# A fused two-block transformer kernel: gates, spreads and mod gates through device memory, aligned small tiles, earlier context rows, later gate work

## The chip, the cores and the metric

The kernel runs on one core of a Trainium2 chip. Five engines work side by side, each through its own queue in order: TensorE (PE, matrix products into PSUM; PEld is its weight load), VectorE (DVE), ScalarE (ACT), GpSimd (POOL) and SyncE (SP, which here issues nearly all transfers between device memory and the on-chip memory SBUF). The metric is the device time of one launch in microseconds; the median of the runs is compared.

## What is computed

Two blocks of two layers each, on 512 rows of 1024 numbers, in float32. The first block mixes tokens by an mLSTM in chunks of 128 with gates per head, beside a sliding-window attention; a convolutional gated network follows. The second block takes a condition vector and 256 context rows, and mixes by pooling, neighbourhood attention with a bias and retention in both directions; a modulated, gated network follows. Cut to what the change touches:

```python
def mlstm_chunkwise(q, k, v, log_i, log_f):          # first block
    ...
    bc = jnp.cumsum(chunks(log_f), axis=-1)
    def step(carry, inp):
        C, n, m = carry
        q_, k_, v_, b_, li_ = inp
        dlog = b_[..., :, None] - b_[..., None, :] + li_[..., None, :]
        dlog = jnp.where(causal, dlog, -jnp.inf)
        inter = b_ + m[..., None]
        m_row = jnp.maximum(inter, jnp.max(dlog, axis=-1))
        w_intra = jnp.exp(dlog - m_row[..., None])
        w_inter = jnp.exp(inter - m_row)
        s = jnp.einsum('bhtd,bhsd->bhts', q_, k_) * w_intra
        ...
        ws = jnp.exp(ls - m_new[..., None])
def token_mixer(h, w_in, qk_conv_w, qk_conv_b, gate_bias, mh_norm_g, attn_sinks, w_out):
    z = h @ w_in
    ...
    log_i = gates[..., :MLSTM_HEADS]
    log_f = jax.nn.log_sigmoid(gates[..., MLSTM_HEADS:])
def modulate(t, shift, scale):                       # second block
    return t * (1 + scale) + shift
def neighborhood_attention(q, k, v, kc, vc, rpb, rows):
    ...
    s_loc = jnp.where(valid, s_loc + bias, NEG_INF)
def retention_chunks(q, k, v, log_gamma, state, with_outputs):
    ...
        s_new = s * c_dec[None, :, None, None] + jnp.einsum('bhcd,bhce->bhde', kb * k_dec[None, :, :, None], vb)
```

## The kernel before

**Products.** A float32 product is done as three products of split numbers (`mm3`, L435 to L437): a high part times a high part, high times low, low times high. Weights stream in: SP fetches a slab into `wr` (3 buffers, L359), ScalarE casts its high part to `wh` (L373), VectorE subtracts to get the low part `wl` (L374); 5 buffers each. Normed rows, turned so that features lie on partitions, stand as `nh` and `nl`. A row of the trace such as `mm<-nh,wh` names the two operands.

**Order.** The program is recorded by a planner: `later(delay, fn)` puts a step on a heap against `s.now`, a count of TensorE's planned nanoseconds, and while the weight products are recorded, the steps that are due are recorded between them. So the delays and the table `Q` of start times set each engine's order, and nothing is reordered on the chip. SP's queue is in order too: a transfer that waits for its data holds all fetches behind it.

**Temporaries.** Nearly every temporary is a tile of the tag `u`: a ring of 34 buffers. Some shapes of 516 and 528 columns use the same tag, so each buffer has 2112 bytes per partition, and a tile's start goes through eight values modulo 512 bytes. `wh`, `wl`, `nh`, `nl` start 32 bytes past a multiple of 512.

**Gates of the mLSTM (`gates`, twice, once a layer).** From 8 gate columns per row, TensorE turns 4x128 tiles (`ax<-ident,t`), VectorE copies them to rows of 4x512 (L910), and makes the running sums and maxima by scans (L918 and L923, with five short steps between and after); TensorE turns two of the results back (`ax<-ident,u` of 4x4 output). In `mlstm`, `spread` brings each head's row to 64 partitions by a matmul with a 0/1 matrix `sel2` (4 rows deep) and takes Exp from PSUM (L1080); `decay` makes a 128x512 matrix from one row by three matmuls (L1101 to L1103: minus the row's high part, minus its low part, plus a causal mask) and takes Exp per chunk (L1108).

**Second block.** `mod` makes the modulation columns `md`; `gate_bc` (6 calls) spreads a gate from columns to rows over all partitions by 16 matmuls each (`ax<-ident,md`) and two ScalarE copies. `early` loads the 256 context rows into `mraw` (L2012) when block two starts, and Norm squares them on ScalarE (L141). The neighbourhood bias comes into `mraw` tiles with a zero half; retention's six state steps (`step`, L1320 and L1321) go in one direction on VectorE and in the other on GpSimd.

Of the kernel before, what the change touches and what calls it, by code (L numbers as in the profile page):

```python
# [11 lines left out]
F32 = mybir.dt.float32  # L12
F32R = mybir.dt.float32r
AF = mybir.ActivationFunctionType
ALU = mybir.AluOpType
# [11 lines left out]
NU = 34  # L27
# [4 lines left out]
NW = 5  # L32
NM = 2
MOD_T = 2330
T_M = 30000
NRAW = 4
# [12 lines left out]
Q = {"swa": 2600, "ctx": 612, "na": 1218, "ret": 6600, "mod": 19000, "mod0": 30000.0, "cn": 18000, "gates": 1750, "fill": 11520, "na1": 1600, "na2": 6253, "na3": 2116, "sw1": 1400, "sw2": 3135, "sw3": 1250, "cx1": 1080, "cx2": 2160, "cx3": 1557}  # L49
# [155 lines left out]
class Net:  # L205
    def __init__(s, ctx, tc, a):
        s.tc, s.nc, s.a = tc, tc.nc, a
        s.sb = ctx.enter_context(tc.tile_pool(name="sb", bufs=1))
        s.ps = ctx.enter_context(tc.tile_pool(name="ps", bufs=1, space=bass.MemoryType.PSUM))
# [5 lines left out]
        s.mready = []  # L215
        s.modon = False
# [83 lines left out]

    def u(s, shape=(P, 512), dt=F32):
        x = s.sb.tile(list(shape), dt, tag="u", name=s.nm("u"), bufs=NU)
        return x
# [9 lines left out]
    def tag(s, tag, shape, bufs, dt=F32):  # L313
        return s.sb.tile(list(shape), dt, tag=tag, name=s.nm(tag), bufs=bufs)
# [318 lines left out]
    def ffn(s, l, up, dn, taps, groups, causal, bias, make_sinks, parts, early=None):  # L633
# [7 lines left out]
        for i in range(np_):  # L641
            f0, f1 = parts[i], parts[i + 1]
            if up == "up2" and i == np_ - 1:
                yield from s.until(lambda: len(s.mready) == 2)
# [4 lines left out]
            if early and i == np_ - 1:  # L649
                yield from s.until(lambda: 0 in s.mready)  # L650
                early()
# [103 lines left out]
    def consts1(s):  # L755
        nc = s.nc
        bf = mybir.dt.bfloat16
        s.identb = s.fix([P, P], "identb", bf)
        nc.vector.tensor_copy(s.identb, s.ident)
# [10 lines left out]
        s.nid4 = s.fix([4, 4], "nid4", F32R)  # L770
        nc.vector.tensor_scalar(out=s.nid4, in0=s.ident[:4, :4], scalar1=-1.0, scalar2=None, op0=ALU.mult)
        s.sel2 = s.fix([4, 2, P], "sel2")
        nc.sync.dma_start(s.sel2, s.a["sel2"])
        s.ones4 = s.fix([4, 512], "ones4")
        nc.vector.memset(s.ones4, 1.0)
        nc.vector.memset(s.ones4.rearrange("p (c t) -> p c t", t=P)[:, :, 0:1], 0.0)
# [7 lines left out]
    def consts3(s):  # L784
        nc = s.nc
        s.cos1 = s.sin1 = s.swm = s.sel2 = None
# [4 lines left out]
        s.bias = []  # L791
        for _ in range(2):
            bias = s.tag("mraw", [P, 1024], NRAW)
            nc.gpsimd.memset(bias, 0.0)
            s.bias += [bias[:, i * 512:i * 512 + 512] for i in range(2)]
# [1289 lines left out]
```

## Time and profile before

| | |
|---|---|
| median of 3 runs | 2862.58 us (2859.92 to 2866.8) |
| the profiled execution | 2865.19 us, of which span 2863.4 us |
| TensorE | 2762.5 us busy, 96% of the span |
| VectorE, ScalarE, GpSimd | 66%, 41%, 20% |
| mean granted TensorE clock | 0.983 of full speed |
| DMA | 300.68 MB, mean 105 GB/s |

TensorE's busy time counts a matmul until its modelled end, so it overlaps with the next one's start; the spacing of starts is what a matmul costs in a row of them. Granted clock 0.50 in a stretch means that the clock was at its lower level (1.2 GHz) all through it, 1.00 at its upper one (2.4 GHz).

### The profile page before, as it was taken

The numbers are of one execution on the slowest core, as the hardware profiler recorded it, in microseconds if no ns is written. First come the engines' busy times: TensorE is split into PE (matmuls) and PEld (weight loads), VectorE is DVE, ScalarE is ACT, GpSimd is POOL, SyncE is SP. The second block draws the span as 40 slices with busy tenths as digits, with TensorE's granted clock in tenths as the row PEclk, the third lists the DMA queues.
The fourth block names the chain that finished last, engine by engine and source line by source line (L and its number), as shares of the span: only waits on it lengthen the run. The fifth ranks groups of instructions, "written<-read, shape, count | busy, mean of one in ns | idle before, by whom it ended". The sixth has DMA issues, their size and how long they took to land.

```text
span 2863.4 us, 39056 instructions
## 1 busy us (share of the span) xinstructions
PE 2762.5 (96%) x14694; PEld 2316.3 (81%) x14694; DVE 1900.0 (66%) x3414; ACT 1175.6 (41%) x2112; POOL 559.0 (20%) x617
## 2 busy tenths in 40 slices
PE   8899999998999999999999999999999999999998
PEld 6678888876678887788788898888888888888887
DVE  6746867686468677767556777777755556664544
ACT  5445333344454333355443633223235443442433
POOL 3112000032120000036134211220202434201011
PEclk9889999999999999999999999999999999999999
DMA  4122544432134444433332333333212322333332
GB/s 162 55 70 89 169 143 129 152 92 81 45 99 141 143 151 137 141 122 99 104 96 77 91 107 114 103 115 116 89 61 80 117 75 73 96 110 96 96 96 66
DMA packets 106324, 300.68 MB, mean 105 GB/s; under 512 B 12180, under 2 KB 18200, under 8 KB 106136
## 3 DMA queue, kind: packets, MB, share of 16 engines
q1 hardware_dynamic: 105560, 297.14, 33.6%
q8 instruction: 116, 1.90, 0.3%
q10 hardware_dynamic: 576, 1.05, 0.1%
q14 instruction: 72, 0.59, 0.1%
HBM read 296.04 MB, written 2.10 MB: 104 GB/s over the span
## 4 chain that ended last, share of the span: by engine, by line
PE 81%; DVE 9%; ACT 4%; issue 2%; POOL 2%; DMA 1%; SPq 0%; POOLq 0%; DVEq 0%; ACTq 0%
PE mm L435 24%; PE mm L437 24%; PE mm L436 24%; PE ax L569 5%; PE ax L565 3%; DVE wl L374 2%; PE ax L577 1%; ACT u L173 1%; ACT wh L373 1%; POOL u L700 1%; DVE mjunk L835 1%; POOL t L560 1%; DVE u L605 1%; DVE u L1209 1%; DMA wr<-in_up_dram 0%
## 5 line engine op out<-in xcount | busy, mean ns | idle before, releaser
L373 ACT CAST wh<-wr 128x1024 fp32r<-128x1024 f32 (+2 forms) x455 | 461.7, 1017 | 598.3 <-PE mm L437 285.9
L435 PE MATMUL mm<-nh,wh 128*128 128x512 f32 (+1 forms) x1776 | 673.1, 379 | 3.6 <-DVE nh L185 3.6
L436 PE MATMUL mm<-nl,wh 128*128 128x512 f32 (+1 forms) x1776 | 667.7, 376 | 0.8 <-DVE nl L186 0.5
L437 PE MATMUL mm<-nh,wl 128*128 128x512 f32 (+1 forms) x1776 | 667.6, 376 | 0.0
L374 DVE TENSOR_TENSOR wl<-wr,wh 128x1024 fp32r<-128x1024 f32 (+2 forms) x455 | 570.7, 1260 | 109.3 <-ACT wh L373 108.9
L435 PE MATMUL mm<-wh,u 128*128 128x512 f32 (+1 forms) x1176 | 464.5, 395 | 6.8 <-ACT u L620 6.8
L605 DVE SCALAR_TENSOR_TENSOR u<-mm,vec,u 128x511 f32<-128x511 f32 (+2 forms) x440 | 305.8, 695 | 238.6 <-ACT u L600 161.8
L436 PE MATMUL mm<-wl,u 128*128 128x512 f32 (+1 forms) x1176 | 458.8, 390 | 2.5 <-DVE wl L374 2.4
L437 PE MATMUL mm<-wh,u 128*128 128x512 f32 (+1 forms) x1176 | 459.1, 390 | 1.4 <-DVE u L621 1.4
L435 PEld LDWEIGHTS mm<-nh,wh 128*128 128x128 f32 x1776 | 336.6, 190 | 66.1 <-issue 4.8
L437 PEld LDWEIGHTS mm<-nh,wl 128*128 128x128 f32 x1776 | 336.7, 190 | 61.0
L436 PEld LDWEIGHTS mm<-nl,wh 128*128 128x128 f32 x1776 | 337.0, 190 | 59.0 <-DVE nl L186 1.0
L435 PEld LDWEIGHTS mm<-wh,u 128*128 128x128 f32 x1176 | 221.8, 189 | 55.8 <-ACT u L620 7.7
L436 PEld LDWEIGHTS mm<-wl,u 128*128 128x128 f32 x1176 | 221.9, 189 | 50.0 <-DVE wl L374 4.4
L437 PEld LDWEIGHTS mm<-wh,u 128*128 128x128 f32 x1176 | 221.4, 188 | 49.4 <-DVE u L621 2.5
L435 PE MATMUL mm<-wh,nh 128*128 128x384 f32 (+2 forms) x512 | 193.6, 378 | 6.1 <-DVE nh L185 5.8
L565 PE MATMUL ax<-ident,u 128*128 128x128 f32 (+1 forms) x946 | 139.7, 283 | 57.3 <-DVE u L152 16.5
L437 PE MATMUL mm<-wh,nl 128*128 128x384 f32 (+2 forms) x512 | 184.0, 359 | 1.3 <-POOL nl L186 1.3
L436 PE MATMUL mm<-wl,nh 128*128 128x384 f32 (+2 forms) x512 | 184.0, 359 | 0.0
L565 PEld LDWEIGHTS ax<-ident,u 128*128 128x128 f32 (+1 forms) x946 | 109.6, 145 | 91.5 <-issue 30.9
L725 POOL TENSOR_TENSOR x<-x,u 128x512 f32<-128x512 f32 x64 | 102.5, 1602 | 352.2 <-DVE u L724 351.4
L560 POOL TENSOR_TENSOR t<-t,mhalf 128x1 f32<-128x1 f32 (+2 forms) x76 | 61.9, 817 | 528.4 <-DVE t L558 528.1
(262 smaller groups left out, 3760.0 us busy)
## 6 DMA issues: line engine op xcount, KB each, us to landing
wr<-in_up_dram SPq DMA_DIRECT2D x176, 512.0 KB, 3.9
mrow<-in_wmod_dram SPq DMA_DIRECT2D x192, 256.0 KB, 2.9
wr<-in_dn_dram SPq DMA_DIRECT2D x88, 512.0 KB, 4.0
wr<-in_wo_dram SPq DMA_DIRECT2D x56, 512.0 KB, 3.6
wr<-in_w2b_dram SPq DMA_DIRECT2D x56, 384.0 KB, 3.1
wr<-in_w2a_dram SPq DMA_DIRECT2D x39, 512.0 KB, 3.6
mraw<-in_nab_dram SPq DMA_DIRECT2D x36, 128.0 KB, 3.5
wr<-in_w1q_dram SPq DMA_DIRECT2D x8, 512.0 KB, 5.1
```

The lines of the kernel that those rows point to most:

```text
L173: nc.scalar.activation(m[:, j, :], src, AF.Identity, scale=n.g[:, k:k + 1], bias=n.b[:, k:k + 1])
L373: nc.scalar.copy(h[:, :n], raw[:, :n])
L374: s.wlo[i] = lambda: nc.vector.tensor_sub(lo[:, :n], raw[:, :n], h[:, :n].bitcast(F32))
L435: mm(ps, ah, bh, start=first, stop=False)
L436: mm(ps, ah, bl, start=False, stop=False)
L437: mm(ps, al, bh, start=False, stop=last)
L560: nc.gpsimd.tensor_tensor(out=r, in0=e, in1=s.mhalf[:, :n], op=ALU.pow)
L565: s.nc.tensor.transpose(out, in_, s.ident[:p, :p])
L569: s.nc.tensor.matmul(out, l, r, start=start, stop=stop, **kw)
L577: s.nc.tensor.matmul(out[q], l, r, start=start, stop=stop, tile_position=(0, i * 64))
L605: nc.vector.scalar_tensor_tensor(out=c[:, o], in0=ps[:, i], scalar=w[q], in1=c[:, o], op0=ALU.mult, op1=ALU.add)
L725: eng.tensor_add(x[:, c], x[:, c], o)
```

## The change

1. **Gates.** They start later (`Q["gates"]` 1750 to 16000). The turns go through device memory: `gates2` stores 8 pieces element by element into `grow`, `gates3` loads two 4x512 rows, `gates4` scans as before (with fewer tiles), `fin` stores five rows into `gfin`, `cols` loads 8 pieces element by element as columns, `ends` takes the Exp.
2. **mLSTM.** `bring` loads rows of `gfin` over 64 partitions, `spread` takes Exp in place; `bring_m` loads a row over 128 partitions, `mask` subtracts it from the causal mask on GpSimd, `decay` takes Exp in place. `sel2`, `nid4`, `identb`, `ones4` go.
3. **Mod gates.** `keep` stores the gate columns once (`mgate`), `gate_bc` loads them over 128 partitions; the two waits for `mready` become waits for `mgate`.
4. **Context rows** are loaded at planned 60000 ns instead of in `early`.
5. **Tiles.** The ring `u` has 31 buffers of 2048 bytes, aligned to 512; a new ring `ub` of 6 takes the wider shapes; `wh`, `wl`, `nh`, `nl` are aligned to 512; the bias tiles get a buffer of their own (`nab`), `mraw` goes from 4 to 2.
6. **Small.** The pads' memsets go from GpSimd to VectorE; the pool sums reuse a tile; `mod`'s scratch is ScalarE's `junk`.

```diff
-NU = 34
+NU = 31
+NB = 6
...
-NRAW = 4
+NRAW = 2
...
-Q = {... "gates": 1750, ...
+Q = {... "gates": 16000, ...
...
     def u(s, shape=(P, 512), dt=F32):
-        x = s.sb.tile(list(shape), dt, tag="u", name=s.nm("u"), bufs=NU)
-        return x
+        n = 1
+        for d in shape[1:]:
+            n *= d
+        if n > 512:
+            return s.sb.tile(list(shape), dt, tag="ub", name=s.nm("ub"), bufs=NB)
+        return s.sb.tile(list(shape), dt, tag="u", name=s.nm("u"), bufs=NU, align_bytes=512)
...
+            def keep():
+                gd = s.dram([2, 2, D], "mgate")
+                for w in range(2):
+                    for i in range(2):
+                        o = (3 * i + 2) * 8
+                        nc.sync.dma_start(gd[w, i].rearrange("(j p) -> p j", p=P), md[:, w, o:o + 8])
+                s.mgate[l] = gd
+            s.later(1200, keep)
...
     def gate_bc(s, l, w, part):
...
-                s.mmf(ps[:, j * P:(j + 1) * P], s.md[l][:, w, o:o + 1].to_broadcast([P, P]), s.ident)
...
-            nc.scalar.copy(g, ps)
+            row = s.mgate[l][w, part // 3, half * 512:half * 512 + 512]
+            s.nc.sync.dma_start(g, row.partition_broadcast(P))
...
-        s.later(6930, lambda: s.gates2(g3, lf3, got))
+        s.later(6000, lambda: s.gates2(g3, lf3, gd, got))
+    def gates2(s, g3, lf3, gd, got):
+        for i, src in enumerate((g3, lf3)):
+            for t in range(NT):
+                nc.sync.dma_start(gd[i * 4:i * 4 + 4, t * P:(t + 1) * P].rearrange("h p -> p h"), src[:, t, :4])
+        s.later(3000, lambda: s.gates3(gd, got))
+    def gates3(s, gd, got):
-            for t in range(NT):
-                s.tr(ps[:4, t * P:(t + 1) * P], src[:, t, :4])
             r = s.u((4, 512))
-            nc.vector.tensor_copy(r, ps[:4, :])
+            nc.sync.dma_start(r, gd[i * 4:i * 4 + 4])
+        s.later(2800, lambda: s.gates4(rows, got))
...
         def fin():
+            gr = s.dram([5, 4, 512], "gfin")
+            for i, x in enumerate((bm, a, m, wi, ws)):
+                nc.sync.dma_start(gr[i], x)
+            s.later(2600, lambda: cols(gr))
+        def cols(gr):
+            co = s.ti(32)
+                    nc.sync.dma_start(co[:, i * 16 + c * 4:i * 16 + c * 4 + 4],
+                                      gr[i, :, c * P:(c + 1) * P].rearrange("h p -> p h"))
+            s.later(2800, lambda: ends(gr, co))
...
+        def bring(hp):
+                    nc.sync.dma_start(w[i * 64:i * 64 + 64, :], gr[src, hp * 2 + i].partition_broadcast(64))
+        def bring_m(hp):
+                nc.sync.dma_start(w, gr[2, hp * 2 + i].partition_broadcast(P))
+            s.later(2800, lambda: mask(hp))
+        def mask(hp):
+                nc.gpsimd.tensor_sub(w, s.cmaskb, w)
         def spread(hp):
-                s.mmf(ps, s.sel2[:, hp, :], src)
-                nc.scalar.activation(w, ps, AF.Exp)
+                nc.scalar.activation(w, w, AF.Exp)
         def decay(h):
-            nc.tensor.matmul(ps, neg, mh, start=True, stop=False)
-            nc.tensor.matmul(ps, neg, ml, start=False, stop=False)
-            nc.tensor.matmul(ps, s.identb, s.cmaskb, start=False, stop=True)
...
+    def load_ctx():
         for i in range(2):
             x = s.tag("mraw", [P, D], NRAW)
             nc.sync.dma_start(x, a["ctx"][i * P:(i + 1) * P])
             cs.append(x)
+    s.later(60000, load_ctx)
```

In the changed program the lines of `mm3` are L447 to L449, transposes are L577 and `step` is L1357 and L1358.

On TensorE, in the mLSTM of layer 0 (`wh`, `wl` are weights, `nh`, `nl` normed rows), this stood before:

```order
L436 MATMUL mm_1459<-wl_1028,nh_109 128x512
L437 MATMUL mm_1459<-wh_1027,nl_110 128x512
L569 MATMUL ax_1468<-u_786,sel_158 128x512
L569 MATMUL ax_1472<-u_785,sel_158 128x512
L435 MATMUL mm_1460<-wh_1027,nh_109 128x512
```

and a little further on

```order
L565 MATMUL ax_1514<-ident_65,u_1495 128x128 x4
L1101 MATMUL ax_1521<-u_914,nid_156 128x512
L1102 MATMUL ax_1521<-u_915,nid_156 128x512
L1103 LDWEIGHTS identb_144
L1103 MATMUL ax_1521<-cmaskb_146,identb_144 128x512
```

After the change, weight products and transposes follow each other there:

```order
L449 MATMUL mm_1428<-wh_983,nl_112 128x512
L577 MATMUL ax_1501<-ident_67,u_1478 128x128 x4
L447 MATMUL mm_1429<-wh_983,nh_111 128x512
L448 MATMUL mm_1429<-wl_984,nh_111 128x512
L449 MATMUL mm_1429<-wh_983,nl_112 128x512
L447 MATMUL mm_1430<-wh_983,nh_111 128x512
```

The four-row matmuls are gone from between the weight products, which moved together.

On VectorE, in the attention stage of layer 0 (L1025 and its L1035, L1036, L581 are softmax steps, L1209 convolution taps), the gate steps L910 to L920 stood before between two of the softmax steps:

```order
L1028 TENSOR_TENSOR t_760<-small_82,t_758 128x2
L910 COPY u_773<-ax_768 4x512
L910 COPY u_780<-ax_775 4x512
L917 MEMSET t_789 4x1
L918 SCALAR_TENSOR_TENSOR u_782<-ones_160,u_780 4x512
L919 TENSOR_TENSOR u_783<-u_773,u_782 4x512
L920 COPY u_788<-u_782 4x3
L374 TENSOR_TENSOR wl_710<-wr_692,wh_709 128x1024
```

The same place after the change, where softmax, split and taps (now L1049, L386, L1246) follow each other:

```order
L1052 TENSOR_TENSOR t_744<-small_84,t_742 128x2
L386 TENSOR_TENSOR wl_694<-wr_676,wh_693 128x1024
L1077 COPY u_763<-ax_760 128x256
L1254 TENSOR_SCALAR u_679<-u_679 128x512
L1246 SCALAR_TENSOR_TENSOR u_770<-mm_681,vec_72,u_770 128x511
L1059 TENSOR_TENSOR t_732<-t_732,t_733 128x2
```

The gate steps stand now behind the last convolution taps of the stage (L1246 writing `u_986`):

```order
L593 TENSOR_SCALAR u_952<-u_952,t_956 128x256
L1246 SCALAR_TENSOR_TENSOR u_986<-mm_872,vec_72,u_986 128x509
L934 MEMSET t_1013 4x1
L935 SCALAR_TENSOR_TENSOR u_1010<-u_1012,u_981 4x512
L936 TENSOR_TENSOR u_979<-u_979,u_1010 4x512
```

On SP, the queue that feeds the weights (`wr`), slab fetches followed each other in this stage before:

```order
L359 DMA wr_1021<-in_w1o_dram 128x1024
L359 DMA wr_1127<-in_w1o_dram 128x1024
L359 DMA wr_1274<-in_wo_dram 128x1024
L359 DMA wr_1360<-in_wo_dram 128x1024
L359 DMA wr_1448<-in_wo_dram 128x1024
```

After the change the gates' stores and loads stand between them (`x4` is four such transfers):

```order
L371 DMA wr_879<-in_w1o_dram 128x1024
L912 DMA grow_821<-t_813 128x4x1 x4
L912 DMA grow_821<-t_815 128x4x1 x4
L371 DMA wr_977<-in_w1o_dram 128x1024
L920 DMA u_979<-grow_821 4x512
L920 DMA u_981<-grow_821 4x512
L371 DMA wr_1084<-in_w1o_dram 128x1024
L950 DMA gfin_1115<-u_1011 4x512
```

The slab fetches keep their order and now stand behind transfers that wait for VectorE.

## Rows read from the trace of the kernel before

**Rows 1.** The page, parts 1 and 4: busy us (share), the chain by engine.

```profile
PE 2762.5 (96%) x14694; PEld 2316.3 (81%) x14694; DVE 1900.0 (66%) x3414; ACT 1175.6 (41%) x2112; POOL 559.0 (20%) x617
...
PE 81%; DVE 9%; ACT 4%; issue 2%; POOL 2%; DMA 1%; SPq 0%; POOLq 0%; DVEq 0%; ACTq 0%
```

**Rows 2.** TensorE by line and shape, whole span: busy us, mean ns, idle.

```profile
L435 PE MATMUL mm<-nh,wh 128*128 128x512 f32 x1520 | 598.8, 394 | 0.0
...
L435 PE MATMUL mm<-wh,u 128*128 128x512 f32 x1080 | 430.1, 398 | 6.8 <-ACT u L620 6.8
```

**Rows 3.** The same view: groups that the change takes off TensorE.

```profile
L569 PE MATMUL ax<-ident,md 128*128 128x128 f32 x96 | 11.6, 276 | 0.0
L569 PE MATMUL ax<-u,sel 4*128 4x512 f32 x16 | 11.5, 854 | 0.0
...
L1101 PE MATMUL ax<-u,nid 4*128 4x512 f32 x8 | 4.6, 574 | 0.0
...
L1102 PE MATMUL ax<-u,nid 4*128 4x512 f32 x8 | 3.6, 448 | 0.0
L1103 PE MATMUL ax<-cmaskb,identb 128*128 128x512 bf16 x8 | 3.6, 444 | 0.0
L565 PE MATMUL ax<-ident,t 128*4 128x128 f32 x16 | 2.1, 272 | 0.0
L565 PE MATMUL ax<-ident,u 4*128 4x4 f32 x16 | 2.0, 245 | 3.7 <-DVE t L1025 3.7
```

**Rows 4.** Timeline of TensorE from 149.4 us: start us, us, line.

```profile
149.62 0.40 PE L436 MATMUL mm<-wl,nh 128*128 128x512 f32 x1
149.86 0.40 PE L437 MATMUL mm<-wh,nl 128*128 128x512 f32 x1
```

**Rows 5.** Stretches: length, busy us of engines, PEclk, DMA share, GB/s.

```profile
150.00:170.00 20.00, 20.00 (x65) 11.14 (x65) 3.02 (x4) 6.01 (x18) 3.39 (x2) 0.57 0.09 27
755.00:770.00 15.00, 15.00 (x38) 8.11 (x36) 3.21 (x4) 5.43 (x11) 3.42 (x2) 0.66 0.13 35
```

**Rows 6.** Waits of TensorE, 64:110, then 668:712: us, times, longest.

```profile
PE ax L565 <- DVE u L581: 6.7, 3, 4.6
PE ax L565 <- DVE t L1025: 3.4, 3, 1.8
...
PE ax L565 <- DVE t L1025: 4.7, 3, 2.6
```

**Rows 7.** Stretches, as Rows 5, in the attention stage of layer 0.

```profile
80.00:85.00 5.00, 0.66 (x2) 0.36 (x2) 4.90 (x11) 0.14 (x1) 0.37 (x1) 0.73 0.00 0
85.00:90.00 5.00, 3.24 (x13) 2.74 (x14) 4.15 (x15) 4.09 (x15) 1.29 (x1) 0.50 0.32 105
115.00:120.00 5.00, 5.00 (x27) 3.78 (x26) 1.31 (x7) 0.59 (x3) 0.57 (x1) 0.86 0.00 0
```

**Rows 8.** Groups of VectorE, 64 to 95 us: gate work of layer 0.

```profile
L910 DVE COPY u<-ax 4x512 f32<-4x512 f32 x2 | 1.3, 670 | 0.0
...
L918 DVE TENSOR_TENSOR_SCAN u<-ones,u 4x512 f32<-4x512 f32 x1 | 1.2, 1212 | 0.0
```

**Rows 9.** Waits of all engines, 1195:1220 us, at context rows.

```profile
ACT junk L141 <- DMA mraw<-in_ctx_dram: 6.4, 1, 6.4
...
PE mm L435 <- ACT u L620: 5.8, 1, 5.8
```

**Rows 10.** DMA issues, 0 to 66 us: KB, us to landing.

```profile
small<-in_rows_dram SPq DMA_DIRECT2D x1, 28.0 KB, 9.9
edge<-in_edge_dram SPq DMA_DIRECT2D x1, 18.0 KB, 2.3
```

**Rows 11.** Timeline: a VectorE, a GpSimd retention step; a wait, 1532:1546.

```profile
1534.75 0.95 DVE L1320 TENSOR_TENSOR u<-u,t 64x384 f32<-64x384 f32 x1
...
1541.27 1.20 POOL L1321 TENSOR_TENSOR u<-u,u 64x384 f32<-64x384 f32 x1
...
PE ax L565 <- DVE u L1440: 3.1, 1, 3.1
```

More of the change, by code (lines that the diff above doesn't have):

```diff
@@ L32 @@
 NW = 5
+ALIGNED = ("wh", "wl", "nh", "nl")
 NM = 2
@@ L790, in consts3 @@
         nc.sync.dma_start(s.sin2, s.a["sin2"])
[L791 to L795, printed above, removed]
+        bias = s.tag("nab", [P, 5, 256], 1)
+        nc.gpsimd.memset(bias[:, 4, :], 0.0)
+        s.bias = [(bias[:, i, :], bias[:, i::4 - i, :]) for i in range(4)]
         s.nbias = 0
@@ L835, in part @@
             nc.vector.tensor_tensor_reduce(
-                out=junk, in0=raw, in1=crow[w], scale=1.0,
+                out=s.junk()[:, :512], in0=raw, in1=crow[w], scale=1.0,
                 scalar=acc[:, w, f:f + 1] if h else s.v("bmod", l, f), op0=ALU.mult, op1=ALU.add,
@@ L873, in gate_bc @@
     def gate_bc(s, l, w, part):
-        nc = s.nc
         out = []
         for half in range(2):
-            ps = s.ax()
-            for j in range(4):
-                o = part * 8 + half * 4 + j
-                s.mmf(ps[:, j * P:(j + 1) * P], s.md[l][:, w, o:o + 1].to_broadcast([P, P]), s.ident)
             g = s.u()
-            nc.scalar.copy(g, ps)
+            row = s.mgate[l][w, part // 3, half * 512:half * 512 + 512]
+            s.nc.sync.dma_start(g, row.partition_broadcast(P))
             out.append(g)
@@ L930, in fin, with ends @@
         def fin():
[L931 to L939 removed]
+            gr = s.dram([5, 4, 512], "gfin")
[4 more added lines that the diff above has]
+            co = s.ti(32)
+            for i in range(2):
+                for c in range(NT):
+                    nc.sync.dma_start(co[:, i * 16 + c * 4:i * 16 + c * 4 + 4],
+                                      gr[i, :, c * P:(c + 1) * P].rearrange("h p -> p h"))
+            s.later(2800, lambda: ends(gr, co))
+        def ends(gr, co):
+            nc.scalar.activation(co[:, :16], co[:, :16], AF.Exp, scale=-1.0)
+            got["gates"] = (co[:, :16], gr, co[:, 16:])
         s.later(1800, stab)
@@ L1909, in layout @@
     out["sin1"] = tok(np.concatenate([-sin, sin], 1))
-    sel2 = np.zeros((4, 2, P), np.float32)
-    for h in range(4):
-        sel2[h, h // 2, (h % 2) * 64:(h % 2) * 64 + 64] = 1.0
-    out["sel2"] = sel2
     w2 = f["w_in_2"]
@@ L2009, in early @@
         s.consts3()
+        hold["c0"] = Norm(s, cs, *s.mcol(0, 1, 0))
+        for t in range(2):
+            s.later(1323 + 2032 * t, lambda t=t: hold["c0"].start(t))
+    def load_ctx():
         for i in range(2):
@@ L2013, in early @@
             cs.append(x)
-        hold["c0"] = Norm(s, cs, *s.mcol(0, 1, 0))
-        for t in range(2):
-            s.later(1323 + 2032 * t, lambda t=t: hold["c0"].start(t))
+    s.later(60000, load_ctx)
     norm = Norm(s, xs, s.v("g_pre_mix", 0, 0, 8))
```

92 lines of the change are left out of this document (45 added, 47 removed).

## The prediction

> **What bounds the kernel now.** I read the page first: which engine is busy, and what the chain that ended last is made of. TensorE is busy for 96% of the span and makes 81% of the chain; VectorE, at 66%, comes into the chain with 9% [rows 1]. So a microsecond counts if it leaves TensorE's queue, ends one of its waits, or lets it run at its upper clock. The groups by line come next, for what each removed kind of matmul costs [rows 2, 3]; the timeline shows that a group's mean is not what a matmul costs in a row of them: it lasts 0.40 us, but the next one starts 0.24 us after it [rows 4]. Then the stretches, for granted clock and for the engine that is full while TensorE waits [rows 5, 7], and the waits themselves [rows 6, 9].
>
> **What goes from TensorE.** The groups taken off are 96 spreads of `md` columns, 16 spreads with `sel`, the 24 matmuls of the decays, and 32 small transposes: 11.6 + 11.5 + 4.6 + 3.6 + 3.6 + 2.1 + 2.0 = 39.0 us busy [rows 3]. A busy sum counts the drain of the last matmul of a block, which the next block covers: 0.40 - 0.24 = 0.16 us [rows 4], for some 28 blocks (12 of `md`, 8 of `sel`, 4 of decays, 4 of transposes) 4.5 us. I take 34.5 us, with 39 and, if half of the blocks only filled waits for others, 17 as the ends. What covers the operations that take their place is looked at below.
>
> **The clock around them.** From 150 to 170 us, where the four-row spreads and decays of layer 0 stand, the granted clock is 0.57 while TensorE is busy all the time; from 755 to 770, in layer 1, it is 0.66 [rows 5]. Against full clock that is 20 x 0.43 = 8.6 and 15 x 0.34 = 5.1 us. About half of each stretch is removed work, whose slowness is in the 34.5 already; the other half is weight products and transposes that stay: 6.9 us. I take 6. The other end is 0: the heads that follow have matmuls of few rows and short length too, and could keep the clock where it is.
>
> **Gate work off a full VectorE.** In layer 0 TensorE waits 6.7 us for softmax results (L581) and 3.4 for L1025, the longest single one 4.6 [rows 6]. Then TensorE has 0.66 us of work in 5, VectorE 4.90 of 5 [rows 7]: VectorE is the bound of this stretch. Its gate steps stand in the middle: two copies, 1.3 us, a scan of 1.2, a second scan as long, and four more short steps of about 0.67 (the copies' mean) [rows 8], in all 1.3 + 1.2 + 1.2 + 4 x 0.67 = 6.4 us. Moved behind the last taps, they meet a VectorE that has 1.31 of 5 us to do [rows 7], so 6.4 of the 10.1 us should go, and the clock, 0.73 in the stall and 0.50 after it, recovers some 5 x 0.50 = 2.5 us. In layer 1 there are 4.7 us of the second kind of wait [rows 6]; by the same share 3 us, and 2 for the clock. Sum: 6.4 + 2.5 + 3 + 2 = 14. The rest of the waits stays, since softmax and split work are not moved. Lower end 0 (softmax steps become late for another reason), upper end 10.1 + 4.7 + 5 = 20.
>
> **Context rows.** ScalarE stands 6.4 us at L141 for the DMA of the context rows, and behind it in its queue is the cast L620, for which TensorE waits 5.8 us [rows 9]. Loaded at planned 60 us, the rows lie ready a millisecond earlier. On SP the two transfers now stand between slab fetches of the attention stage, where DMA is idle for two thirds and more [rows 7], in front of five split buffers: nothing. What is late next is VectorE's half of the same split, which took 0.7 of those 5.8 us after ScalarE. I take 6: 5.8, a little clock behind the stall, less that. The ends are 4 and 8.
>
> **Alignment.** Two groups of equal size differ only in operands: weights as the one operand that comes from `nh`, 394 ns, and from the ring `u`, 398 ns [rows 2]. The tiles of `u` start at eight places modulo 512 bytes, those of `nh` at one. If equal starts are what makes the 4 ns, 3 x 1080 matmuls x 4 ns = 13 us are there to be had. I take 10, with 0 and 13 as the ends of this reading; that the start itself, not its change, costs something is a rival.
>
> **What is added.** (a) *Hops through device memory.* No row shows a 4-byte store. The nearest are a 28 KB load in 56-column pieces while the start is crowded, 9.9 us, and an 18 KB one of 36 columns in quiet, 2.3 us [rows 10]. The chain of a layer has five hops, with planned waits of 2.6 to 3 us: covered if a hop takes 2.3, and late by 5 x 7 = 35 us at 9.9. The stage is quiet as it was for the second (DMA share 0.00 to 0.32 [rows 7]), so I take that row, and 3 us for both layers for ScalarE standing at an Exp while a load lands; the ends are 0 and, with the slack before the heads, 30. The Trainium skill, "DMA: Bandwidth & Descriptors", section "Anatomy of one DMA", puts the fixed cost of a transfer at about 2 us, mostly the receipt, which would make the price of these hops nothing; the quiet row's 2.3 us is in line with it, and no run so far shows a store of this kind. (b) *Queues.* SP holds stores that wait for VectorE in front of slab fetches; three raw and five split buffers are queued ahead of TensorE, so I cost it at nothing. If a store is late by more than these buffers cover, TensorE stands for the weights. (c) *GpSimd's masks,* eight subtractions of 128x512, stand where its share of 3.4 in 20 us [rows 5] leaves room: nothing, or 2 us if the heads wait. (d) *The tighter ring.* 31 buffers for nearly all temporaries, where 34 were. The place where it can bite is retention: six steps run on VectorE and six on GpSimd side by side, from 1534.75 to 1542.47 us (the last starts at 1541.27 and lasts 1.20), and right after them TensorE waits 3.1 us for VectorE's L1440 [rows 11]. If a temporary of the one chain is the buffer of the other's last one, the chains take turns, and the 7.7 us become up to twice that, less what falls together now: 6 us more in each layer. I take 4 a layer, and 4 for the rest of the ring: 12. The ends are 0 and 25. (e) *Small ones* (12 row loads for the mod gates, due long before use, pads' memsets on VectorE, the shared scratch, bias tiles): 1, at most 3.
>
> **The sum.** 34.5 + 6 + 14 + 6 + 10 = 70.5 gained; 3 + 12 + 1 = 16 lost; 54.5 net. The profiled execution of before took 2865.2 us, 2.6 over the median of 2862.6. 2862.6 - 54.5 = 2808.1: I forecast **2808 us**.
>
> **Rivals.** *The waits stay, and only the matmuls go.* VectorE bounds the attention stage with softmax alone, and alignment gives nothing: 34.5 + 6 - 16 = 24.5 gained, with the context rows: 2862.6 - 24.5 - 6 = 2832 us. For it: VectorE is still 4.15 of 5 us busy after the stall [rows 7]. Against: the gate steps stand right in the stall. 0.15.
> *The ring bites.* Turns of two engines in retention and late buffers elsewhere at their upper end of 25, and half of the removed work refilled by waits: 70.5 - 17 - 25 - 4 = 24.5 gained, 2838 us. For it: wait right behind the chain [rows 11]. Against: three buffers of 34, and the wide shapes have a ring of their own now. 0.08.
> *Slower: the chain through device memory is late.* The element-wise stores and loads (16 a layer, each of 512 pieces of 4 bytes) take the crowded 9.9 us a hop, not 2.3 [rows 10]; the five hops of a layer end 35 us late, and both the heads, and the slab fetches queued behind the stores, wait for them. It decides from the point at which a layer's chain is later by more than half of the net gain, 27 us; at 35, and a clock lost behind each stall, it costs 2 x 36 = 72 instead of 3 us, and 54.5 gained turn to 54.5 + 3 - 72 = 14.5 lost: 2877 us. Against: the quiet row. 0.07. The Trainium skill, "DMA: Bandwidth & Descriptors", section "Specifications", asks for at least 512 B in a piece for line rate and says that below it the engine reads, modifies and writes; that speaks for this rival, and no row of before shows a store of such pieces.
> *A start on 512 bytes makes every matmul cheaper.* Matmuls of 512 columns start 0.24 us apart [rows 4]; at 2.4 GHz the columns alone are 0.213. If half of the difference (13 ns) comes from starts 32 bytes off, the 3 x (1520 + 1080) matmuls of [rows 2] give 100 us, and the time is 2862.6 - 44.5 - 100 = 2718 us. Nothing in the profile speaks for it but that difference. 0.08.
>
> **How the numbers follow.** Forecast 0.62, its own range 2788 to 2828 (the stage's and the ring's ends). Waits stay 0.15, ring 0.08, slower 0.07, starts 0.08. Leaving out the slow rival and most of the large gain, the range is **2775 to 2848**. A measurement of this kernel can tell about 0.2%, 5.7 us, from no change. Slower by more than that takes the slow rival, less a little where its chain is late by about the net gain: 0.06; within it falls that part and the far end of the ring's rival: 0.04; faster 0.90.
>
> **What the profile after should show.** Groups with `sel`, `nid`, `identb`, and `md` as an operand gone from TensorE, about 39 us of busy time; granted clock near 0.8 or more where 0.57 and 0.66 were; no wait for L581 of over 2 us before the first products of values; no wait for `mraw` at ScalarE's L141; the group of `wh` with `u` at the mean of that with `nh`. Wrong would be: a wait of TensorE for ScalarE's Exp or GpSimd's mask at the heads (hops late); waits for slabs `wr` in the attention stage (SP held); VectorE's retention steps waiting for GpSimd one by one, with TensorE's wait behind them at 9 us instead of 3 (ring); unchanged means of 394 and 398 (alignment).

## The result: 2814.6 us, 1.8% faster

The changed kernel took 2814.55 us (median of 4 runs, 2813.32 to 2815.41), the kernel before 2864.69 us in the runs beside it; the ratio is 0.9823 (95% interval 0.9803 to 0.9844). Forecast were 2808 us within 2775 to 2848. The profiled execution has a span of 2811.5 us where before had 2863.4: 51.9 us less.

Of the page of the changed kernel, the row on busy time, which answers to the first of [rows 1]:

```profile
PE 2705.4 (96%) x14526; PEld 2291.8 (82%) x14526; DVE 1895.9 (67%) x3414; ACT 1167.0 (42%) x2098; POOL 572.0 (20%) x616
```

TensorE is still 96% busy, so it is still the bound, with 57 us less of busy time. The seven groups of [rows 3] are gone from it; of those with `sel` only groups 128 rows deep are left, which stood in the kernel before too. Of the groups of TensorE by line and shape, the two that answer to [rows 2] (mean ns is the number before the second bar):

```profile
L447 PE MATMUL mm<-nh,wh 128*128 128x512 f32 x1520 | 597.5, 393 | 0.0
...
L447 PE MATMUL mm<-wh,u 128*128 128x512 f32 x1080 | 425.2, 394 | 1.9 <-ACT u L632 1.9
```

The group of `wh` with `u`, in which the tile of `u` is the stationary operand (the one that is loaded as weights), now takes what the group of `nh` with `wh` takes, in which `wh` is the stationary one: 394 and 393 ns, where they took 398 and 394.

The waits of TensorE in the attention stages, 60 to 125 us (layer 0) and then 640 to 735 us (layer 1), answer to [rows 6] (us in total, times, longest):

```profile
PE mm L447 <- DVE t L934: 5.4, 1, 5.4
PE ax L589 <- ACT u L1075: 3.2, 2, 2.1
PE ax L589 <- DVE t L1049: 1.8, 1, 1.8
...
PE mm L447 <- DVE t L934: 5.4, 1, 5.4
PE ax L589 <- ACT u L1075: 3.7, 3, 3.0
```

The waits for softmax (L581 and L1025 of before, L593 and L1049 now) are down to 2.0 us in layer 0, but a new one of 5.4 us stands in each layer: by the order of the instructions TensorE waits there for a PSUM bank, which the last convolution taps on VectorE free; the releaser that is named, L934, is the next instruction on VectorE (in e9, below, it is the tap itself). The first tap, L1243 on ScalarE, stands behind a weight cast there, as ScalarE's timeline shows:

```profile
96.45 1.04 ACT L385 CAST wh<-wr 128x1024 fp32r<-128x1024 f32 x1
97.39 0.78 ACT L1243 ACTIVATE u<-mm,vec 128x512 f32<-128x512 f32 x1
```

All waits of the layer 0 window sum to 11.5 us, where before had 13.2.

The stretch of the mLSTM in layer 0, 130 to 175 us, in the same columns as [rows 5], first in the kernel before, then in the changed one:

```profile
130.00:175.00 45.00, 45.00 (x232) 30.29 (x229) 15.35 (x35) 19.43 (x49) 6.26 (x10) 0.81 0.12 36
```

```profile
130.00:175.00 45.00, 43.65 (x295) 35.20 (x294) 24.51 (x59) 24.41 (x66) 13.70 (x16) 1.00 0.34 95
```

The granted clock (the number after the GpSimd count) is 1.00 where it was 0.81, with some more idle time on TensorE. In layer 1, from 740 to 780 us, it is 1.00 where it was 0.87. ScalarE no longer waits for the context rows as in [rows 9]; their transfers start at 73 us (first and last start at the end of the numbers):

```profile
L2050 SPq DMA_DIRECT2D mraw<-in_ctx_dram x2: 423/424/426, 73.0 to 73.5; - x2
```

Two things grew. The turns through device memory are slow, as SP's own instructions (start us, us), its wait among them, the stretch from 79 to 95 us and the four microseconds from 83 to 87 us in it show:

```profile
79.01 12.29 SPq L912 DMA_DIRECT2D grow<-t  x8
...
97.86 3.90 SPq L920 DMA_DIRECT2D u<-grow  x2
...
SPq L912 <- DMA wr<-in_w1o_dram: 6.9, 1, 6.9
...
79.00:95.00 16.00, 12.13 (x61) 9.04 (x61) 10.43 (x33) 9.69 (x26) 4.68 (x4) 0.79 1.17 35
...
83.00:87.00 4.00, 2.19 (x14) 1.77 (x15) 1.77 (x7) 3.96 (x12) 0.00 (x0) 0.50 1.35 1
```

From the first to the last of the eight element-wise stores of one layer SP takes 12.29 us, 6.9 of them a wait that the profile puts down to a slab fetch. All DMA engines are taken (the share 1.17, and 1.35 from 83 to 87 us) while they move next to nothing (1 GB/s from 83 to 87 us), and the loads of the rows can start only at 97.86: the hop takes 18.9 us. And retention's two chains take turns: timeline of VectorE, of GpSimd, and the wait of TensorE behind them, which answer to [rows 11]:

```profile
1488.56 0.55 DVE L1357 TENSOR_TENSOR u<-u,t 64x384 f32<-64x384 f32 x1
1489.15 0.55 DVE L1358 TENSOR_TENSOR u<-u,u 64x384 f32<-64x384 f32 x1
1491.79 0.55 DVE L1357 TENSOR_TENSOR u<-u,t 64x384 f32<-64x384 f32 x1 [2.09 <-POOL u L1358]
...
1489.84 0.83 POOL L1357 TENSOR_TENSOR u<-u,t 64x384 f32<-64x384 f32 x1 [1.80 <-DVE u L1358]
1490.75 1.00 POOL L1358 TENSOR_TENSOR u<-u,u 64x384 f32<-64x384 f32 x1
...
PE ax L577 <- DVE u L1477: 5.1, 1, 5.1
```

VectorE does its step, GpSimd waits for it, does its own, and VectorE waits 2.09 us for that. TensorE's wait behind them is 5.1 us where it was 3.1. From the first of VectorE's steps to the end of the last the chains take 11.2 us, where they took 7.7.

### The profile page after: what moved, and what is told of

It reads as the page before. It is cut to its first block, busy times and chain, and to the rows that moved or that the text cites. A ratio compares the mean times of both kernels' runs of the same rounds, so it can differ in the third digit from the quotient of the medians.

```text
span 2811.5 us, 38854 instructions
## 1 busy us (share of the span) xinstructions
PE 2705.4 (96%) x14526; PEld 2291.8 (82%) x14526; DVE 1895.9 (67%) x3414; ACT 1167.0 (42%) x2098; POOL 572.0 (20%) x616
## 5 line engine op out<-in xcount | busy, mean ns | idle before, releaser
L447 PE MATMUL mm<-nh,wh 128*128 128x512 f32 (+1 forms) x1776 | 671.6, 378 | 3.6 <-DVE nh L187 3.6
L449 PE MATMUL mm<-nh,wl 128*128 128x512 f32 (+1 forms) x1776 | 665.9, 375 | 0.0
L386 DVE TENSOR_TENSOR wl<-wr,wh 128x1024 fp32r<-128x1024 f32 (+2 forms) x455 | 572.3, 1263 | 112.5 <-ACT wh L385 112.1
L447 PE MATMUL mm<-wh,u 128*128 128x512 f32 (+1 forms) x1176 | 460.5, 392 | 2.1 <-ACT u L632 1.9
L449 PE MATMUL mm<-wh,u 128*128 128x512 f32 (+1 forms) x1176 | 454.4, 386 | 2.2 <-DVE u L633 1.5
L447 PEld LDWEIGHTS mm<-nh,wh 128*128 128x128 f32 x1776 | 336.6, 190 | 66.3 <-issue 4.8
L449 PEld LDWEIGHTS mm<-nh,wl 128*128 128x128 f32 x1776 | 336.0, 189 | 60.4
L447 PEld LDWEIGHTS mm<-wh,u 128*128 128x128 f32 x1176 | 221.9, 189 | 46.8 <-ACT u L632 2.7
L449 PEld LDWEIGHTS mm<-wh,u 128*128 128x128 f32 x1176 | 221.6, 188 | 46.0 <-DVE u L633 3.5
L447 PE MATMUL mm<-wh,nh 128*128 128x384 f32 (+2 forms) x512 | 191.1, 373 | 17.2 <-DVE t L934 10.8
L577 PE MATMUL ax<-ident,u 128*128 128x128 f32 x930 | 137.4, 283 | 50.6 <-DVE u L154 18.3
L449 PE MATMUL mm<-wh,nl 128*128 128x384 f32 (+2 forms) x512 | 182.0, 355 | 1.5 <-POOL nl L188 1.5
L577 PEld LDWEIGHTS ax<-ident,u 128*128 128x128 f32 x930 | 108.5, 144 | 80.9 <-issue 25.0
```

Source lines behind the costliest of these rows:

```text
L386: s.wlo[i] = lambda: nc.vector.tensor_sub(lo[:, :n], raw[:, :n], h[:, :n].bitcast(F32))
L447: mm(ps, ah, bh, start=first, stop=False)
L449: mm(ps, al, bh, start=False, stop=last)
L577: s.nc.tensor.transpose(out, in_, s.ident[:p, :p])
```

## Experiments

Each experiment is compared with kernels that were timed beside it; differences of 2 or 3 us between medians are not told apart by these runs, and then the rows decide or the point stays open. The granted clock differs from run to run of one kernel, too: of the kernel before, the 23 runs beside e9 go from 2853.44 us at a mean clock of 0.989 to 2876.78 us at 0.979, about 2.4 us for each 0.001. Where it matters, a run's span times its mean clock is given below as a rough estimate of what the same work would take at the upper level; rough, since TensorE's waits at the lower level are counted in it as well.

### The tiles

e1 gives the changed kernel the ring and the starts of before:

```diff
-NU = 31
+NU = 34
...
-ALIGNED = ("wh", "wl", "nh", "nl")
+ALIGNED = ()
...
-        n = 1
...
-        return s.sb.tile(list(shape), dt, tag="u", name=s.nm("u"), bufs=NU, align_bytes=512)
+        x = s.sb.tile(list(shape), dt, tag="u", name=s.nm("u"), bufs=NU)
+        return x
```

> The changed kernel with the tiles of before: one ring of 34 buffers of 2112 bytes for all temporaries, starts at eight places modulo 512, wh, wl, nh, nl 32 bytes past a multiple of 512. If the change of starts is what made the 4 ns, the three groups of wh with u go back from 394, 390 and 390 ns to 398, 394 and 394, which is 13 us; the wait behind retention goes back from 5.2 to 3.1 us in each layer, which gives 4 us: about 2823 us. If alignment did nothing and only the ring got tighter, the groups stay and the time is 2810 us or less.

Measured: 2819.73 us (ratio 0.9829, 0.9804 to 0.9854). The three groups of TensorE with `u` as the stationary operand (L443, L444 and L445 are the three products of `mm3` here), and its wait behind retention:

```profile
L443 PE MATMUL mm<-wh,u 128*128 128x512 f32 x1080 | 430.5, 399 | 1.7 <-ACT u L628 1.7
L445 PE MATMUL mm<-wh,u 128*128 128x512 f32 x1080 | 426.3, 395 | 1.8 <-DVE u L629 1.8
L444 PE MATMUL mm<-wl,u 128*128 128x512 f32 x1080 | 426.2, 395 | 1.2 <-DVE wl L382 1.2
...
PE ax L573 <- DVE u L1473: 6.1, 2, 3.0
```

The 512-column group is back at 399 ns, 5.3 us more than the 425.2 of the changed kernel; with its two partners it is 15.6 us. Against it stands the wait behind retention, which falls from 10.3 to 6.1 us in both layers. The 256-column groups, in which `u` is the moving operand, are 1 or 2 ns quicker, and those of 384 columns with `u` as the stationary one take no more either (358, 340 and 339 ns; 369, 349 and 348 in the changed kernel). Of 15.6 - 4.2 = 11.4 us, 5.5 were measured against the next run, on the same chip; the rest is within what two such medians can differ by (the mean clock of e1's runs is 0.9892, that of e2's 0.9875), or in the waits elsewhere.

e2 keeps the rings, but drops the alignment, so that every buffer of `u`, `wh`, `wl`, `nh` and `nl` starts at 416 modulo 512:

```diff
-ALIGNED = ("wh", "wl", "nh", "nl")
+ALIGNED = ()
...
-        return s.sb.tile(list(shape), dt, tag="u", name=s.nm("u"), bufs=NU, align_bytes=512)
+        return s.sb.tile(list(shape), dt, tag="u", name=s.nm("u"), bufs=NU)
```

> The changed kernel without the alignment to 512, in the same rings: every buffer of u, wh, wl, nh and nl starts at 416 modulo 512, 32 past a multiple of 64. If it is the change of starts from one weight load to the next that costs, all starts are still equal and nothing moves: 2814 us, groups of wh with u at 394, 390, 390. If the start itself costs, the groups go back to 398, 394, 394 or more, and the time is 2826 us or more.

Measured: 2814.26 us (0.9804, 0.9780 to 0.9828), and

```profile
L447 PE MATMUL mm<-wh,u 128*128 128x512 f32 x1080 | 425.7, 394 | 1.9 <-ACT u L632 1.9
```

Nothing moves. So the start at 512 by itself is worth nothing: one common start for all of these tiles, 0 or 416, gives 394, 390 and 390 or 391 ns, the ring of before with its eight starts 4 to 5 ns more. The rival with 100 us falls. How the old ring costs this is not shown. That the start changes from one stationary tile to the next doesn't explain it alone: `mm3` loads the same tile for its first two products, so nothing changes before L444 of e1, and its group has risen as much as the others. In e1 the stationary tiles also start elsewhere than the moving ones (`wh` and `wl` at 32), in e2 and in the changed kernel at the same place; no run parts this reading from the other.

### The matmuls that went

e3 puts the mod gates back on TensorE:

```diff
-            s.later(1200, keep)
+            s.mgate[l] = 1
...
-            row = s.mgate[l][w, part // 3, half * 512:half * 512 + 512]
-            s.nc.sync.dma_start(g, row.partition_broadcast(P))
+            ps = s.ax()
+            for j in range(4):
+                o = part * 8 + half * 4 + j
+                s.mmf(ps[:, j * P:(j + 1) * P], s.md[l][:, w, o:o + 1].to_broadcast([P, P]), s.ident)
...
+            s.nc.scalar.copy(g, ps)
```

> The changed kernel with the mod gates spread again by 96 matmuls with md and copied by ScalarE; no stores and loads of mgate. By the sum, the 96 matmuls come back on the path: 11.6 us busy less a drain for each of 12 blocks, about 10 us: 2824 us. If TensorE only filled waits with them, or the loads cost as much: 2815 us.

Measured: 2824.46 us (0.9841, 0.9817 to 0.9866), 10.2 over e2 on the same chip. The group is back as it was:

```profile
L581 PE MATMUL ax<-ident,md 128*128 128x128 f32 x96 | 11.6, 276 | 0.0
```

11.6 us busy, 10.2 in the time: about what the drain leaves (12 blocks at 0.16 us [rows 4] take 1.9 off).

e4 puts the mLSTM's spreads and decays back on TensorE, with one buffer of the ring less (30):

```diff
-NU = 31
+NU = 30
...
+            for src, dst in ((ws, wsb), (wi, wib)):
+                ps = s.ax()
+                s.mmf(ps, s.sel2[:, hp, :], src)
...
+                nc.scalar.activation(w, ps, AF.Exp)
...
-            for w in (wsb[hp], wib[hp]):
-                nc.scalar.activation(w, w, AF.Exp)
...
-            w = dec[h]
+            ps = s.ax()
...
+            nc.tensor.matmul(ps, neg, mh, start=True, stop=False)
+            nc.tensor.matmul(ps, neg, ml, start=False, stop=False)
+            nc.tensor.matmul(ps, s.identb, s.cmaskb, start=False, stop=True)
...
```

> The changed kernel with the mLSTM's spreads (16 matmuls with a 0/1 matrix) and decays (24 matmuls) on TensorE again, from the gate rows as the changed kernel makes them; the ring has one buffer less for the two small matrices. By the sum it loses 23.3 us of busy time less some 2 of drain and about 6 for the clock: 2841 us, and the granted clock falls to about 0.6 again for some 20 us in each layer. If the clock does not follow these matmuls, 2835 us and no such stretch; if they only filled waits, 2820 us.

Measured: 2839.64 us (0.9895, 0.9874 to 0.9916), 25.4 over e2. The spreads' group, the mLSTM's stretch, the wait behind retention, and the stretch around that wait in the first layer of block two, here and (last) in e2:

```profile
L581 PE MATMUL ax<-u,sel 4*128 4x512 f32 x16 | 7.9, 613 | 0.0
...
130.00:175.00 45.00, 44.75 (x287) 33.38 (x288) 20.73 (x59) 23.44 (x63) 7.30 (x12) 1.00 0.17 48
...
PE ax L577 <- DVE u L1472: 17.8, 2, 8.9
...
1470.00:1560.00 90.00, 78.41 (x487) 71.41 (x487) 51.77 (x83) 24.53 (x40) 37.08 (x43) 0.94 0.23 74
...
1470.00:1560.00 90.00, 82.14 (x500) 73.04 (x499) 62.75 (x106) 32.68 (x58) 36.29 (x39) 0.96 0.26 78
```

The size was as expected, but not for the reason that was expected: the clock is 1.00 with all these matmuls in place, and a spread takes 613 ns, not the 854 of [rows 3]. What fills the sum, as far as the traces show, is the ring: with 30 buffers the wait behind retention is 17.8 us instead of 10.3, that is 7.5 of the 25.4, and 17.9 are left. The clock takes some more: it is 0.94 in both of these stretches, where e2 has 0.96 and 0.98, and over all runs of the two kernels the mean is 0.9864 and 0.9875, an estimated 3.5 to 5 us. So the matmuls by themselves cost 13 to 18 us, the more the less of this is put down to the ring. No run has the matmuls with 31 buffers, so this division is read from waits and clock and not tested by itself.

### The gate work

e5 starts the gate work of the changed kernel early again, `"gates": 16000` to `"gates": 1750`:

> The changed kernel with the start of the gate work put back from 16000 to 1750. By the step of the prediction (gate work off a full VectorE, 14 us) the time goes to 2828 us and TensorE's waits for softmax between 70 and 90 us are back at 8 us in layer 0. The trace after speaks for less: TensorE waits some 12 us there in either kernel, since the gates' logarithm with its two table loads and the taps behind a softmax now stand in the stage; then 2818 us or less.

Measured: 2828.89 us (0.9868, 0.9844 to 0.9892), 17.3 over e6 (below), which ran on the same chip, and 14.3 over the median of the changed kernel. VectorE's first scan, TensorE's wait, and the mLSTM's stretch:

```profile
87.00 1.21 DVE L935 TENSOR_TENSOR_SCAN u<-u,u 4x512 f32<-4x512 f32 x1 [7.34 <-DMA u<-grow]
...
PE ax L589 <- DVE t L1049: 7.3, 1, 7.3
...
130.00:175.00 45.00, 43.30 (x306) 34.73 (x306) 24.93 (x64) 23.68 (x65) 12.99 (x16) 1.00 0.35 104
```

VectorE stands 7.34 us for the row from device memory, and TensorE waits 7.3 us for the softmax step that is queued behind it. The clock is lower, too, from 90 to 130 us 0.83, where the changed kernel has 0.91; the mean of e5's runs is 0.9852, that of e6's 0.9892, an estimated 11 us, which overlap with the waits. In the mLSTM it is 1.00, though the gate work is early; the spreads and decays are not on TensorE in e5. So the late start is needed here because of the hops, and the number of the prediction came out for another reason. Whether the late start does anything by itself, e9 shows: the kernel before, with that one number changed.

> The kernel before with the start of the gate work alone put from 1750 to 16000, its turns still on TensorE. The step of the prediction on this (a full VectorE) gives 14 us: 2851 us. The waits in the trace after, 11.5 us in layer 0 where 13.2 were and 12.5 in layer 1 where 12.9 were, say that the move by itself brings next to nothing, and that the 14 us which the early start costs with the hops is the price of waiting for rows from device memory: 2862 us.

Measured: 2857.77 us (0.9973, 0.9958 to 0.9989), 6.5 less than before. The mLSTM's stretch, the one ahead of it here and then in the kernel before, and two waits of e9 from 60 to 125 us:

```profile
130.00:175.00 45.00, 44.34 (x283) 31.92 (x283) 20.16 (x56) 22.95 (x63) 7.86 (x11) 1.00 0.16 48
...
90.00:130.00 40.00, 31.60 (x177) 23.74 (x176) 29.41 (x85) 14.30 (x46) 8.80 (x10) 0.81 0.14 40
...
90.00:130.00 40.00, 34.34 (x200) 25.33 (x200) 27.55 (x85) 17.36 (x54) 7.33 (x11) 0.88 0.13 40
...
PE mm L435 <- DVE u L1209: 8.0, 1, 8.0
PE ax L577 <- ACT u L1051: 3.0, 1, 3.0
```

TensorE's waits in the stage do not shrink: 14.3 us where 13.2 were, the taps' wait being 8.0. In layer 1 they are 14.3 us too, where 12.9 were. In e9 the gate steps stand on VectorE in front of the last taps (they end at 100.7 us, the taps start at 101.28), in the changed kernel behind them; so the placement is not quite the same, and the wait for the taps is 8.0 us here and 5.4 there. What changes is the mLSTM, which runs at clock 1.00 instead of 0.81 (1.00 instead of 0.87 in layer 1), with the same spreads and decays on TensorE. Part of that comes back ahead of it: from 90 to 130 us the clock is 0.81, where before had 0.88. The runs agree that e9's gain is the clock: its mean is 0.9865 in 12 runs, where the 23 of before have 0.9843, and span times clock is 2817 us in both.

e6 takes the gates' logarithm out of the late part, and e7 makes the first turn on TensorE (with the scans at about the same planned time):

```diff
 e6: "gates": 1750 and
-        s.later(6000, lambda: s.gates2(g3, lf3, gd, got))
+        s.later(20250, lambda: s.gates2(g3, lf3, gd, got))
 e7: in gates2
...
-                nc.sync.dma_start(gd[i * 4:i * 4 + 4, t * P:(t + 1) * P].rearrange("h p -> p h"), src[:, t, :4])
+                s.tr(ps[:4, t * P:(t + 1) * P], src[:, t, :4])
...
+            nc.vector.tensor_copy(r, ps[:4, :])
...
```

> The changed kernel with the bias, Abs, Exp, Log steps of the gates at 1750 again and only the stores and what follows them late, as in the changed kernel. If the two table loads of 1.28 us and VectorE's wait of 2.15 us for the logarithm at 79 to 81 us are what TensorE waits for right after (1.95 and 2.26 us), 3 us in each layer go: 2808 us. If softmax is the bound there anyway, 2814 us.

> The changed kernel with the first turn of the gates (columns to rows) by TensorE's eight small transposes and two copies per layer again, at the same planned time, and the rest through device memory; the 16 stores of 512 pieces of 4 bytes are gone. They hold SP for 12 us in each layer and the DMA engines are busy in every slice from 79 to 95 us. If anything waits for that (slabs, the scans' rows), the time falls by up to 10 us, to 2805; the transposes and copies cost 1 us a layer. If all of it is covered, 2816 us.

Measured: e6 2811.61 us (0.9809, 0.9786 to 0.9833), e7 2812.32 us (0.9809, 0.9785 to 0.9833). In e7, from 79 to 95 us and in the waits:

```profile
79.00:95.00 16.00, 12.08 (x60) 9.04 (x61) 10.22 (x34) 9.65 (x24) 4.69 (x4) 0.79 0.22 66
...
PE mm L447 <- DVE u L1251: 4.5, 1, 4.5
```

The DMA engines are busy for 0.22 of that stretch instead of 1.17, and the wait for the bank is still 4.5 us. So the slow stores are covered: almost nothing waited for them once the gates start late. e6's 2811.61 us lies between its two expectations, and TensorE's waits from 60 to 125 us are 10.2 us in it and 11.5 in the changed kernel: the logarithm's part is not told apart from nothing.

### Retention's steps

e8 gives the products of the state steps one buffer of their own, `stt`:

```diff
-NB = 6
+NB = 5
...
-        t = s.u((P, 384))
...
+        t = s.stt
```

> The changed kernel with one buffer of its own for the products of retention's state steps, in place of a buffer of the ring for each (a buffer of the wide ring pays for it). If the tighter ring makes the steps of VectorE and GpSimd take turns, TensorE's wait behind them goes from 5.2 to 3 us or less in each layer and the time to 2810 us; the two engines' chains take 7.7 us side by side again. If the longer wait comes from elsewhere, it stays at 5.2 and the time at 2814 us.

Measured: 2812.31 us (0.9806, 0.9781 to 0.9830). A step of VectorE, one of GpSimd beside it, and the wait:

```profile
1489.07 1.07 DVE L1359 TENSOR_TENSOR stt<-u,t 64x384 f32<-64x384 f32 x1
...
1488.70 1.03 POOL L1359 TENSOR_TENSOR stt<-u,t 64x384 f32<-64x384 f32 x1
...
PE ax L577 <- DVE u L1479: 6.4, 2, 3.2
```

The chains run side by side again and the wait is back at 3.2 us in each layer: the engines took turns because both chains drew this tile from the tighter ring. It cost TensorE 2 us of waiting a layer; the times, 2812.31 and 2814.55 us, are not told apart.

### The context rows

e10 is the kernel before with the rows loaded at planned 60000 by `load_ctx`, as in the change; the gates start early in it.

> The kernel before with the context rows alone loaded at planned 60000. By the prediction 6 us: the wait of 5.8 us goes, 2859 us where the runs of before have 2865; the cast of the same split stays late by other work: 4 us if the 1.9 us of the trace after stay here too.

Measured: 2859.19 us (0.9985, 0.9971 to 1.0000): 5 us, at the edge of what these runs can tell. In the rows, TensorE's wait for the cast behind the squares, in all 6.8 us before, with 5.8 the longest [rows 9], is now the first of these two; the second is the mLSTM's stretch:

```profile
PE mm L435 <- ACT u L620: 2.7, 3, 1.0
...
130.00:175.00 45.00, 44.19 (x236) 29.98 (x234) 14.90 (x37) 20.12 (x53) 6.80 (x10) 0.81 0.13 36
```

The wait is 4.1 us shorter. e10's runs also had a higher clock than the 23 of before, 0.9853 against 0.9843 in the mean; span times clock is 2 us less. So 2 to 5 us are found. The second row serves e9 as a control: with the gate work at its early start, the mLSTM is at clock 0.81 again in this trace.

### All three mends

e11 has the edits of e6, e7 and e8 together; e12 has the turn and the scans 4000 planned ns later.

> The changed kernel with the three mends that were each worth 2 or 3 us: the logarithm of the gates early and the scans late, the first turn by TensorE, and a buffer of their own for retention's steps. If they add, 2814.5 - 3 - 2 - 2 = 2807 us; if the attention stage is bound by softmax and taps in any case, the first two give 3 together: 2809 us.

> The same with the first turn and the scans 4000 planned ns later. If the wait of 4.5 to 5.4 us behind the last convolution taps has the scans in front of it, it falls: 2804 us. If it is the taps themselves (ScalarE's first tap behind a cast), nothing moves or the heads wait for the gates: 2807 us or more.

Measured: 2809.64 us (0.9811, 0.9789 to 0.9833) and 2812.70 us (0.9821, 0.9800 to 0.9842). The median of e11 is 5 us below the changed kernel's, but the intervals overlap nearly whole: not shown to be better. e12's 2812.70 us is no gain either. One wait that none of the mends takes away is TensorE's for the bank behind the taps, 5.1 us in each layer of e11, and 5.4 and 6.4 in e12, though the scans stand later there: it is the taps that TensorE waits for, not the scans.

## Why the prediction held, step by step

**What goes from TensorE: 34.5 forecast, 23 to 28 found.** e3 gives 10.2, and e4 13 to 18 after the parts of the ring and the clock; the transposes were cheap (e7 put 16 of the 32 back without a loss), the other 16 were not tried. The term took the spreads at the 854 ns of a slowed clock, and that belongs to the next step.

**The clock around them: the step that holds only in part.** The prediction laid the 0.57 of [rows 5] on the four-row matmuls. With the same matmuls the clock is 1.00 in e4, and in e9, where only the gate work's start differs from before; so they don't bring it down by themselves, and their removal was not needed. e5 shows the other side: with the gate work early and these matmuls gone, the clock is 1.00 too. In these traces the mLSTM's clock falls only where both stand, the matmuls on TensorE and the gate work at its early start (before, e10); without either it stays up, and the kernel takes away both. That is one trace for each, and e5 differs from before in the rest of the change as well. What was gained there is real (45 x 0.19 = 8.6 us of clock in layer 0, and 40 x 0.13 = 5.2 in layer 1). Why it takes both stays open: in the kernel before TensorE had been busy at its upper level until 150.6 us, and in e9 it is busy without a break from 131.7 to 157.9 us and the clock stays up. The size was too small. Over the whole span the mean clock is 0.983 before and 0.989 after in the profiled executions, 49 and 31 us lost at the lower level by the prediction's way of counting, so of the 51.9 us some 18 come with the clock; the prediction's clock terms were 6 + 2.5 + 2 = 10.5. And some of it differs from run to run of one kernel.

**Gate work off a full VectorE: right in sign, wrong in mechanism.** 14 us forecast, 6.5 found in e9, and none of it from the waits that the step was made of: these rose from 13.2 to 14.3 us there. In the changed kernel, where the gate steps stand behind the taps, they are 11.5 (13.2 before) and 12.5 us (12.9 before), 2.1 us less in both layers together. The step failed where it said that the rest of the waits stays: softmax waits went, and a wait for the last taps took their place, because the taps stand behind the same queue of softmax and casts. VectorE had not been the only full engine: the first tap of ScalarE stands behind its own copies and a weight cast.

**Context rows: 6 forecast, 2 to 5 found** (e10), with an interval that reaches to nothing.

**Alignment: 10 forecast; 15.6 found in the groups, of which 5.5 with the ring's 4.2, so some 10, in the time (e1).** The size is right. Of the reading that was taken, equal starts against differing ones, e2 shows one half: the start itself gives nothing. That the change of start is what costs is not shown (L444 of e1 speaks against it), and the two groups that the prediction compared differ in more than the tile: `u` is the stationary operand of the one, `wh` that of the other, so that both came to 394 ns does not show one cause for both.

**What is added.** The hops were taken at the quiet row's 2.3 us, and a hop of eight element-wise stores takes 18.9 us, more than the bad end of 9.9. The rival that was slower by this had its price too low and its cover too small: the chain has room from 79 us to the heads, so TensorE has no wait for it when it starts late (VectorE stands 2.1 us for the row), and waits 7.3 us when it stands in the middle of the softmax (e5). The other signs of being wrong did not come: from 100 to 175 us TensorE waits neither for slabs nor for an Exp or a mask; the nearest is 1.4 us for VectorE's product with a spread row (L1124). The Trainium skill, "DMA: Bandwidth & Descriptors", section "Specifications", with its 512 B for line rate and read-modify-write below, speaks of such pieces; that they are slow the trace agrees, with the DMA engines taken from 83 to 87 us at 1 GB/s, and what an engine does meanwhile no run here shows. The fixed 2 us of the section "Anatomy of one DMA", measured there for transfers that GpSimd issues, is no price for these, which SP issues: the hop took 18.9 us. The ring's term was right in mechanism (the chains take turns) and too large: 2 us a layer, not 4, since a step is quicker when its neighbour stands still. Of the 4 us for the rest of the ring no wait of the trace shows anything.

**The sum.** 23 to 28 for the matmuls, 6.5 for the late start with its clock, 2 to 5 for the context rows and 5.5 for the tiles, ring included, make 37 to 45 of the 50.1 us. These were measured from two sides (some by undoing, some alone), so they need not add; which part the remaining 5 to 13 belong to is open; the clock's own spread from run to run is of that size. The forecast of 54.5 came close in part by luck: an overstated gain in waits and matmuls stood against an understated gain in clock and an overstated price of the ring.

## What to carry to other kernels

Work taken off a bound engine at full clock gave about its spacing (e3); a mean from a stretch at the lower clock overstates it, and the clock itself can come back by moving something else, so that what took it down is named only after each change has been tried without the other. Two kernels whose clocks differ are compared over several runs, since the clock of one kernel differs from run to run. A turn through device memory in 4-byte pieces is cheap only if its whole 19 us stand beside other work: before one moves it, the question is what is queued behind the instruction that waits for it. When buffers get fewer, look for two engines that draw from one ring in turn.

## What was not expected of the hardware

Half a state step of retention, one instruction, takes 0.55 us on VectorE while GpSimd stands still, and 1.07 beside it; on GpSimd the two halves take 0.83 and 1.00 against 1.03 and 1.20. So taking turns, which could double the chain on paper, makes 11.2 us of its 7.7, and TensorE's wait 2 us longer. The Trainium skill, "SBUF — State Buffer", section "Who interferes with whom", says that a VectorE instruction with two SBUF inputs contends with a GpSimd instruction that reads SBUF; these rows agree.

TensorE's matmuls of 512 columns with a tile of the ring as the stationary operand take 4 to 5 ns more from the old ring, whose buffers start at eight places modulo 512 bytes (e1), than with one common start, be it 0 or 416 (the changed kernel, e2). What it is in the old ring that costs this stays open.

The granted clock of one kernel is not a constant: the 23 runs of the kernel before beside e9 had means from 0.979 to 0.989, and the time followed them over 23 us.
